# A fused encoder layer: the first scores, masks and copies of its short batch issued in another order

## The chip, the cores and the metric

The kernel runs on one core of a Trainium2 chip. The metric is the time of one execution in microseconds (us) on the device. Three executions of the kernel before took 2205.14, 2201.33 and 2206.42 us; the median is 2205.14. The profile was taken in another execution, of 2202.51 us; its span, from the first to the last instruction of the program, is 2200.7 us.

Five engines appear in the profile. PE multiplies matrices (PEld is its loading of weights, which runs beside it). DVE, ACT and POOL work on tiles element by element. SP issues DMAs, and POOL issues some of them too. The order of the instructions of an engine is fixed when the program is built.

## The reference, cut to what matters

One encoder layer runs on two batches with the same weights: 1024 tokens (called A below) and 512 tokens (called B). Per batch:

```
h = rms_norm(x, pre_w);  cols = h @ w_in            # 12304 columns
y_m = o * headnorm(mlstm_fwd + mlstm_bwd) * silu(z)   # 4 heads x 256
y_a = mix of 3 dilated window attentions * silu(z)    # 3 groups x 8 heads x 64
merged = sig(g_A) * (y_m @ w_pm) + sig(g_B) * (y_a @ w_pa)
y = x + rms_norm(merged @ w_out, post_w)
```

The mLSTM is linear attention with gates, here cut into chunks of 128 tokens. For a chunk the reference forms the scores `q k^T`, multiplies them by `exp` of a log weight under a triangular mask, multiplies by `v`, and divides by a row sum. It does so forwards and backwards for each head.

## The kernel before

All data are float32. A product is made of three matmuls (`mm3`, L212 to L214) on operands of the type float32r: each operand x is stored as a high part `hi`, a rounded copy made by ACT, and a low part `lo = x - hi`, made by DVE or POOL. The product is hi\*hi + hi\*lo + lo\*hi. Wherever a matmul needs a new operand, two instructions on two other engines come ahead of it, one after the other.

**Stages.** The program goes through the projections of A (to about 960 us in the trace), then through five stages, each of which has its own small matmuls and a stream of big ones beside it. The stages are the mLSTM of A (`mlstm`), the attention of A (`attend`), the mLSTM of B (`quad`, from about 1587 to 1775 us), the attention of B, and the end. The big matmuls (tile `dense`) belong to projections of B and to the output products of A and B. They are handed out by `Fill`: `fill(share)` issues so many steps, and a step is one `mm3` over 512 columns. `fill.stage(steps, shares)` sets the rate at the start of a stage as steps divided by shares. For `quad` there are 192 steps (`STEPS[2]`). Eight steps use one weight tile, which was split into `wh` (ACT, L275) and `wl` (DVE, L281) two units ahead, in `split_w`. `self.held` is a list of instructions behind which these splits are queued.

**Who sets the order.** PE's order is written out by hand in all of the program, SP's in the five later stages. ACT, DVE and POOL get theirs from a scheduler that simulates the program when it is built, and takes instructions by its own times and by program order. `tc.issue_after(x)` queues the block's instructions of x's engine behind x on that engine; it is no wait between engines.

**The first projection** (`value_group` with g = 0, and `combos`). A matrix product of halves is arranged in seven products (Strassen's way). The first, `m1`, has four PSUM banks; `put(B21, k)` makes the operand of the second for k = 0 to 3: transposes on PE (L423), a high copy on ACT (L430), and a `rest()` that lets PE subtract the high part in PSUM (L436) and ACT copy what remains (L437). When `m1` is done, ACT copies its four banks to `u2[t]` (L588), and the second product is added onto the same banks.

**The mLSTM of B** (`quad`). B has four chunks per head. There are 32 rounds (h, i, d): four heads, four positions, two directions. All scores between chunks of a head are kept in `st`: `prepare(h)` first copies q into `qs` as high and low part (L1321, L1322), splits the keys of chunk 0 into `kh` (ACT, L1314) and `kl` (DVE, L1315), and then, for each chunk c, multiplies (`sc`, six matmuls), splits the next chunk's keys and copies the scores to `st` (L1330). The tiles `kh` and `kl` have one buffer each.

`front(k)` makes the operand of round k: POOL masks a row of logs (L1351, `affine_select`), ACT takes `exp` (L1353), DVE multiplies by scores (L1358, L1359), ACT makes the high part `sch` (L1366) and POOL the low part `scl` (L1367). In between, POOL carries forward the products of the column factors, `cols` (L1364), which read the same row tile `rw`, loaded by a DMA that POOL issues (L253). `core(k)` multiplies with v (`num`, L1380 the high part, L1383 the low one) and normalises. Backwards rounds (d = 1) start with the last chunk, so round 1 of a head needs the scores of chunk 3.

The opening of `quad` is, in program order: `fill(2)`; `prepare(0)` from end to end with `fill(1/5)` after each of its five parts; `front(0)`; then the rounds. Round k calls, in this order, the next part of `prepare` of the next head if one is under way, the row loads, `front(k+1)`, a share of fill, and `core(k)`, which holds two more shares. Preparing the next head begins in the fourth round of a head, so its four score products stand in the fifth to the eighth round.

**The attention of A** (`attend`) has 12 units of 8 rounds. The loads of the next unit are put in a list at the second round of a unit; `spread(n)` sets how many of them each round's `tick` issues on SP, so that the list is empty after n rounds; n is 7.

Of the kernel before, what the change touches and what calls it, by code (L numbers as in the profile page):

```python
# [22 lines left out]
F32 = mybir.dt.float32  # L23
# [160 lines left out]
class Net:  # L184
# [182 lines left out]
    def combos(self, ps, H, xt, r, junk, pw, plus, minus, again, diag):  # L367
# [47 lines left out]
        def put(m, k):  # L415

            if m == T4 and k == 0:
                again()
            p = banks.pop((B21, k)) if m == B22 else ps.tile([P, BLK], F32, name="d")
            banks[m, k] = p  # L420
            begun = m in turned
            for t in range(4) if begun else ():
                nc.tensor.matmul(p[:, t * P:(t + 1) * P], turned[m][t][:, k * P:(k + 1) * P], self.ident, is_transpose=True,  # L423
                                 start=t == 0, stop=True, skip_group_check=True)
            for of, one in others.get(m, ()):
                for x in range(2):
                    nc.tensor.matmul(p, one, H[x][of][:, k], start=not begun, stop=True, skip_group_check=True)
                    begun = True
            hi, lo = H[0][m][:, k], H[1][m][:, k]
            nc.scalar.activation(hi, p, AF.Copy)  # L430
            if m not in (B21, B22):
                self.low = nc.vector.tensor_sub(lo, p, hi.bitcast(F32))  # L432
                return None

            def rest():
                nc.tensor.matmul(p, minus, hi, start=False, stop=True, skip_group_check=True)  # L436
                nc.scalar.activation(lo, p, AF.Copy)  # L437
            return rest

        return lead, norm, sub, put  # L440
# [11 lines left out]
    def value_group(self, g, T, H, sb, us, co, ps, late=None, begin=None, u3=None, more=None, turn=None):  # L452
# [70 lines left out]
        if g == 0:  # L523
# [61 lines left out]

            m1 = product(B11, w11, with_m1(), True)
            for t in range(4):
                nc.scalar.activation(u2[t], m1[t][:, :VW], AF.Copy)  # L588
            w12 = low.pop(0)
            with self.tc.issue_after(low[0]):  # L590
                last = self.sums(wa, wb, s)
# [684 lines left out]
    def quad(self, T, fill, steps, first, after, beside):  # L1276
# [10 lines left out]
        with ExitStack() as stack:  # L1287
# [15 lines left out]
            hacc = x0[:, :n * 256].rearrange("p (n c) -> p n c", c=256)  # L1303
            G = x0[:, 2 * S:4 * S].rearrange("p (c s) -> p c s", c=2)
            qs = [z.rearrange("p (c s) -> p c s", c=2) for x in [self.take("X1")] for z in (x[:, :2 * S], x[:, 2 * S:4 * S])]
            fill.stage(steps, lead + len(rounds) + n // 4 + late + 3)

            def prepare(h):
                self.need(("qk", h))
                x = head[h]  # L1310
                def keys(c):
                    k = x["k"][:, :, c * P:(c + 1) * P]
                    kk = [sb.tile([P, 2, P], F32R, name=z, bufs=1) for z in ("kh", "kl")]
                    nc.scalar.activation(kk[0], k, AF.Copy)  # L1314
                    nc.vector.tensor_sub(kk[1], k, kk[0].bitcast(F32))  # L1315
                    return kk

                with ExitStack() as st_:
                    for z in self.behind if h == 0 else self.acc[:1]:
                        st_.enter_context(self.tc.issue_after(z.ins))  # L1320
                    nc.scalar.activation(qs[0], x["q"], AF.Copy)  # L1321
                    nc.vector.tensor_sub(qs[1], x["q"], qs[0].bitcast(F32))  # L1322
                    kk = keys(0)
                yield
                for c in range(n):
                    p = psum("sc")
                    for ct in range(2):
                        self.mm3(p, [z[:, ct] for z in kk], [z[:, ct] for z in qs], ct == 0, ct == 1)
                    kk = keys(c + 1) if c < n - 1 else None
                    self.turned = nc.scalar.activation(st[h % 2][:, c], p, AF.Copy)  # L1330
                    yield

# [9 lines left out]
            def front(k):  # L1342
# [5 lines left out]
                scores = lambda c1: st[h % 2][:, c1, c * P:(c + 1) * P]  # L1348
                rm = sb.tile([P, n, P], F32, name="rm", bufs=1)[:, :i + 1]
                sg = 1 if d == 0 else -1  # L1350
                nc.gpsimd.affine_select(out=rm[:, i], in_=rw[:, 0], pattern=[[sg, P]], compare_op=OP.is_ge, fill=-NEG, base=0,  # L1351
                                        channel_multiplier=-sg)
                nc.scalar.activation(rm[:, i], rm[:, i], AF.Exp, scale=-1.0, bias=of(0, c))  # L1353
                if i == 0:
                    col[d] = sb.tile([P, 4], F32, name=f"cols{d}")
                for j in range(i):
# [3 lines left out]
                if 0 < i < n - 1:  # L1360
                    e = P - 1 if d == 0 else 0
                    for j in range(i):
                        w = of(1, chunk(j)) if j == i - 1 else col[d][:, j:j + 1]
                        nc.gpsimd.tensor_tensor(col[d][:, j:j + 1], w, rw[:, 1, e:e + 1], op=OP.mult)  # L1364
                hi, lo = (sb.tile([P, n, P], F32R, name=x)[:, :i + 1] for x in ("sch", "scl"))
                nc.scalar.activation(hi, rm, AF.Copy)  # L1366
                nc.gpsimd.tensor_sub(lo, rm, hi.bitcast(F32))  # L1367
                made[k] = hi, lo, of(2, c), [chunk(j) for j in range(i + 1)]

# [52 lines left out]
                rows(0, d)  # L1422
            self.need(("v", 0))
            load_G(0)
            fill(lead)
            for _ in prepare(0):
                fill(1 / 5)
            front(0)
            hold, coming = self.turned, None
            for k, (h, i, d) in enumerate(rounds):  # L1430
                self.tick()
# [19 lines left out]
                    load_G(h)  # L1451
                fill(1 / 3)
                core(k)
                self.sum = self.acc[1]
                next(beside, None)
            self.scans = []
# [327 lines left out]
    def attend(self, T, fill, steps, first, banks, outs, after=None, beside=None, at=()):  # L1784
# [5 lines left out]
        with ExitStack() as st:  # L1790
# [55 lines left out]
            for i in range(12):  # L1846
                now = coming
                for j, t in enumerate(now):
                    if j == 1:
                        if i < 11:  # L1850
                            coming = ready(i + 1)
                            self.spread(T.n - 1 if i or T.n > 4 else 1)
                        elif after:
                            after()
                            self.spread(T.n + 1)
# [629 lines left out]
```

## Time and profile before

| | |
|---|---|
| median of three executions | 2205.14 us (2201.33 to 2206.42) |
| the profiled execution | 2202.51 us |
| its span | 2200.7 us |
| mean granted clock of TensorE | 0.998 |
| DVE, ACT, POOL busy | 66%, 49%, 32% of the span |
| matmuls | 11962 |
| HBM read, written | 274.70 MB, 113.44 MB |

The profile's times are counted from the start of the span. In a timeline a row gives the start, the duration, the engine, the line of the kernel, the operation, the tiles (written <- read), partitions by elements with types, how many instructions were merged, and in brackets how long the engine had been idle before and what ended that. Matmuls overlap: the duration of one (0.39 us at 512 columns) is longer than the distance from its start to the start of the next (0.23 us), so the distance between starts is what a matmul costs. A stretch of several matmuls is thus read by its starts.

### The profile page before, as it was taken

The numbers are of one execution on the slowest core, as the hardware profiler recorded it, in microseconds if no ns is written. First come the engines' busy times: TensorE is split into PE (matmuls) and PEld (weight loads), VectorE is DVE, ScalarE is ACT, GpSimd is POOL, SyncE is SP. The second block draws the span as 40 slices with busy tenths as digits, with TensorE's granted clock in tenths as the row PEclk, the third lists the DMA queues.
The fourth block names the chain that finished last, engine by engine and source line by source line (L and its number), as shares of the span: only waits on it lengthen the run. The fifth ranks groups of instructions, "written<-read, shape, count | busy, mean of one in ns | idle before, by whom it ended". The sixth has DMA issues, their size and how long they took to land.

```text
span 2200.7 us, 34421 instructions
## 1 busy us (share of the span) xinstructions
PE 2181.6 (99%) x11962; PEld 1885.7 (86%) x11962; DVE 1463.0 (66%) x2970; ACT 1087.8 (49%) x2246; POOL 700.6 (32%) x994
## 2 busy tenths in 40 slices
PE   9999999999999999999999999999999999999998
PEld 8999888888888888888888889998778888888887
DVE  7765565657787555547888765564667845666673
ACT  7322243344444343446777666666755544554332
POOL 1000432333333222326677640011044422232331
PEclk9999999999999999999999999999999999999999
DMA  3742443423333222366746569996778786776773
GB/s 126 195 115 78 154 166 134 172 105 115 106 115 113 76 79 96 134 237 218 224 154 215 150 196 251 250 240 192 213 225 274 242 268 209 230 254 189 236 240 106
DMA packets 207641, 390.43 MB, mean 177 GB/s; under 512 B 37513, under 2 KB 121161, under 8 KB 207466
## 3 DMA queue, kind: packets, MB, share of 16 engines
q1 hardware_dynamic: 176584, 276.15, 39.9%
q0 software_dynamic: 27280, 99.48, 14.3%
q10 hardware_dynamic: 3602, 12.59, 1.4%
q8 instruction: 95, 1.56, 0.3%
q14 instruction: 80, 0.66, 0.1%
HBM read 274.70 MB, written 113.44 MB: 176 GB/s over the span
## 4 chain that ended last, share of the span: by engine, by line
PE 92%; DMA 3%; DVE 2%; issue 1%; ACT 1%; SPq 0%; POOL 0%; DVEq 0%; POOLq 0%; ACTq 0%
PE d L214 14%; PE d L212 14%; PE d L213 14%; PE dense L212 12%; PE dense L214 11%; PE dense L213 11%; PE lg L1678 2%; PE pt L1708 1%; PE o L1751 1%; PE num L212 1%; PE num L214 1%; PE num L213 1%; PE num L1380 1%; PE a L1096 1%; PE kv L212 1%
## 5 line engine op out<-in xcount | busy, mean ns | idle before, releaser
L212 PE MATMUL dense<-H,wh 128*128 128x512 f32 x664 | 269.9, 407 | 0.0
L214 PE MATMUL dense<-H,wl 128*128 128x512 f32 x664 | 261.2, 393 | 0.0
L213 PE MATMUL dense<-H,wh 128*128 128x512 f32 x664 | 261.1, 393 | 0.0
L214 PE MATMUL d<-Hh,phla 128*128 128x512 f32 x608 | 236.7, 389 | 0.0
L212 PE MATMUL d<-Hh,phla 128*128 128x512 f32 x608 | 236.7, 389 | 0.0
L213 PE MATMUL d<-Hl,phla 128*128 128x512 f32 x608 | 236.7, 389 | 0.0
L281 DVE TENSOR_TENSOR wl<-wraw,wh 128x1024 fp32r<-128x1024 f32 (+1 forms) x121 | 149.8, 1240 | 58.4 <-ACT wh L275 58.3
L214 PE MATMUL d<-Hh,phlb 128*128 128x512 f32 x456 | 177.5, 389 | 0.0
L212 PE MATMUL d<-Hh,phlb 128*128 128x512 f32 x456 | 177.5, 389 | 0.0
L213 PE MATMUL d<-Hl,phlb 128*128 128x512 f32 x456 | 177.5, 389 | 0.0
L275 ACT ACTIVATE wh<-wraw 128x1024 fp32r<-128x1024 f32 (+1 forms) x124 | 128.3, 1036 | 68.3 <-PE dense L213 25.1
L214 PEld LDWEIGHTS dense<-H,wl 128*128 128x128 f32 x664 | 125.1, 188 | 28.1
L696 POOL TENSOR_TENSOR psum_w<-pw_raw 128x512 f32<-128x512 f32 x38 | 57.3, 1508 | 277.5 <-DMA pw_raw<-w_in 254.2
L214 PE MATMUL d<-vhi,Hl 128*128 128x322 f32 x448 | 140.6, 314 | 0.5 <-DVE Hl L432 0.3
L212 PE MATMUL d<-vhi,Hh 128*128 128x322 f32 x448 | 140.4, 313 | 0.1
L212 PEld LDWEIGHTS dense<-H,wh 128*128 128x128 f32 x664 | 125.6, 189 | 16.7 <-issue 1.2
L213 PE MATMUL d<-vlo,Hh 128*128 128x322 f32 x448 | 139.7, 312 | 0.0
L213 PEld LDWEIGHTS dense<-H,wh 128*128 128x128 f32 x664 | 125.8, 189 | 14.9
L214 PEld LDWEIGHTS d<-Hh,phla 128*128 128x128 f32 x608 | 114.2, 188 | 23.7
L213 PEld LDWEIGHTS d<-Hl,phla 128*128 128x128 f32 x608 | 114.2, 188 | 23.6
L212 PEld LDWEIGHTS d<-Hh,phla 128*128 128x128 f32 x608 | 114.2, 188 | 23.6
L1697 DVE CUSTOM_DVE_ANT_0 ls<-lg,bias 128x256 f32<-128x256 f32 (+2 forms) x240 | 78.7, 350 | 79.1 <-PE lg L1678 52.8
(635 smaller groups left out, 5807.5 us busy)
## 6 DMA issues: line engine op xcount, KB each, us to landing
pw_raw<-w_in SPq DMA_DIRECT2D x76, 512.0 KB, 4.1
wraw<-w_in SPq DMA_DIRECT2D x63, 512.0 KB, 4.6
aqk_a<-pwk SPq DMA_DIRECT2D x40, 512.0 KB, 3.3
wraw<-w_pm POOLq DMA_DIRECT2D x24, 512.0 KB, 5.7
wraw<-w_out POOLq DMA_DIRECT2D x24, 512.0 KB, 3.9
aqk_b<-sw SPq DMA_DIRECT2D x40, 256.0 KB, 5.2
wraw<-w_v POOLq DMA_DIRECT2D x22, 430.0 KB, 6.6
qk_a<-pwk SPq DMA_DIRECT2D x16, 512.0 KB, 2.6
```

The source lines that it names most:

```text
L212: nc.tensor.matmul(out, lh, rh, start=start, stop=False, **kw)
L213: nc.tensor.matmul(out, lh, rl, start=False, stop=False, **kw)
L214: nc.tensor.matmul(out, ll, rh, start=False, stop=stop, **kw)
L275: high = nc.scalar.activation(hi[:, :n], raw[:, :n], AF.Copy)
L281: low = (self.lows or nc.vector).tensor_sub(lo[:, :n], raw[:, :n], hi[:, :n].bitcast(F32))
L696: self.nc.gpsimd.tensor_add(s[:, 0], ws[1][:, 0], ws[1][:, 1])
L1096: nc.tensor.matmul(p[:, c - c0], kT[:, ct, c * P:(c + 1) * P], qT[:, ct, c * P:(c + 1) * P], start=ct == 0, stop=ct == 1)
L1380: nc.tensor.matmul(pn, hi[:, j], z[:, c1], start=j == 0 and z is v[0], stop=False)
L1678: nc.tensor.matmul(lg[:, hh], q[hh][:, qs], z.rearrange("p (n j) -> p n j", j=P)[:, pair], start=z is k[hh], stop=z is not k[hh])
L1697: nc.vector.tensor_tensor_reduce(out=ls[rows, hh], in0=ts["lg"][hh][rows, of], in1=bt[rows, hh, by], scale=1.0, scalar=NEG, op0=OP.add, op ...
L1708: nc.tensor.transpose(pp[:, hh * nk + x], ts["ls"][:, hh, x * P:(x + 1) * P], self.ident)
L1751: nc.tensor.matmul(of(hh, 0, P), vh(kt[x], hh), pt[:, hh * len(kt) + x], start=x == 0, stop=x == len(kt) - 1)
```

## The change

- In `combos` and `value_group`: the copies of banks 1 to 3 of `m1` are queued on ACT behind the last low copy of B21; that of bank 0 is left free.
- In `quad`, `prepare` is taken apart. `kh` has two buffers (the pool's own number), `kl` keeps one, and the high part of the next keys is queued ahead of a chunk's matmuls instead of behind them. For heads 1 to 3 an empty round is put in, so that the four score products stand in rounds 6, 7 and 8 of a head and in round 1 of the next.
- For head 0 the opening is now: first part of `prepare`; `fill(2 + 3/5)`; scores of chunk 0; `fill(1/5)`; `front(0)`; the three other chunks with `fill(1/5)` after each; `fill(1)`; then the rounds. From `front(0)` to the end of the first `core`, the weight splits are queued behind the `exp`, the product and the high part of `front(0)` (`self.held`). The stage's shares are 42 instead of 41.
- In `front`, the column products (L1364) are queued on POOL behind the mask (L1351) of the same front.
- In `attend` for A, the loads of the next unit are spread over 6 rounds instead of 7 (for B, as before).

```diff
-                nc.scalar.activation(lo, p, AF.Copy)
+                self.copied = nc.scalar.activation(lo, p, AF.Copy)
...
             for t in range(4):
-                nc.scalar.activation(u2[t], m1[t][:, :VW], AF.Copy)
+                with self.tc.issue_after(self.copied.ins) if t else ExitStack():
+                    nc.scalar.activation(u2[t], m1[t][:, :VW], AF.Copy)
...
-            fill.stage(steps, lead + len(rounds) + n // 4 + late + 3)
+            fill.stage(steps, lead + len(rounds) + n // 4 + late + 4)
...
-                def keys(c):
-                    k = x["k"][:, :, c * P:(c + 1) * P]
-                    kk = [sb.tile([P, 2, P], F32R, name=z, bufs=1) for z in ("kh", "kl")]
-                    nc.scalar.activation(kk[0], k, AF.Copy)
-                    nc.vector.tensor_sub(kk[1], k, kk[0].bitcast(F32))
-                    return kk
+                of = lambda c: x["k"][:, :, c * P:(c + 1) * P]
+                def high(c):
+                    k = sb.tile([P, 2, P], F32R, name="kh")
+                    nc.scalar.activation(k, of(c), AF.Copy)
+                    return k
+                def low(c, hi):
+                    k = sb.tile([P, 2, P], F32R, name="kl", bufs=1)
+                    nc.vector.tensor_sub(k, of(c), hi.bitcast(F32))
+                    return hi, k
...
-                    kk = keys(0)
+                    kk = low(0, high(0))
                 yield
+                if h:
+                    yield
                 for c in range(n):
+                    coming = high(c + 1) if c < n - 1 else None
                     p = psum("sc")
                     for ct in range(2):
                         self.mm3(p, [z[:, ct] for z in kk], [z[:, ct] for z in qs], ct == 0, ct == 1)
-                    kk = keys(c + 1) if c < n - 1 else None
+                    kk = coming is not None and low(c + 1, coming)
                     self.turned = nc.scalar.activation(st[h % 2][:, c], p, AF.Copy)
                     yield
...
-                nc.gpsimd.affine_select(...)
-                nc.scalar.activation(rm[:, i], rm[:, i], AF.Exp, scale=-1.0, bias=of(0, c))
+                select = nc.gpsimd.affine_select(...)
+                self.fronts = [nc.scalar.activation(rm[:, i], rm[:, i], AF.Exp, scale=-1.0, bias=of(0, c))]
...
-                        nc.gpsimd.tensor_tensor(col[d][:, j:j + 1], w, rw[:, 1, e:e + 1], op=OP.mult)
+                        with self.tc.issue_after(select.ins):
+                            nc.gpsimd.tensor_tensor(col[d][:, j:j + 1], w, rw[:, 1, e:e + 1], op=OP.mult)
...
-                nc.scalar.activation(hi, rm, AF.Copy)
+                self.fronts += [*self.state, nc.scalar.activation(hi, rm, AF.Copy)]
...
-            fill(lead)
-            for _ in prepare(0):
+            scores = prepare(0)
+            next(scores)
+            fill(lead + 3 / 5)
+            next(scores)
+            fill(1 / 5)
+            front(0)
+            self.held = self.fronts
+            for _ in scores:
                 fill(1 / 5)
-            front(0)
+            fill(1)
...
                 core(k)
+                self.held = []
...
-                            self.spread(T.n - 1 if i or T.n > 4 else 1)
+                            self.spread(T.n - (2 if T.n > 4 else 1) if i or T.n > 4 else 1)
```

More of the change, by code (lines that the diff above doesn't have):

```diff
@@ L1350, in front @@
                 sg = 1 if d == 0 else -1
-                nc.gpsimd.affine_select(out=rm[:, i], in_=rw[:, 0], pattern=[[sg, P]], compare_op=OP.is_ge, fill=-NEG, base=0,
-                                        channel_multiplier=-sg)
-                nc.scalar.activation(rm[:, i], rm[:, i], AF.Exp, scale=-1.0, bias=of(0, c))
+                select = nc.gpsimd.affine_select(out=rm[:, i], in_=rw[:, 0], pattern=[[sg, P]], compare_op=OP.is_ge, fill=-NEG, base=0,
+                                                 channel_multiplier=-sg)
+                self.fronts = [nc.scalar.activation(rm[:, i], rm[:, i], AF.Exp, scale=-1.0, bias=of(0, c))]
                 if i == 0:
```

## The prediction

> **What bounds the kernel now.** I read the page first, then the list of who PE waited for, then PE's timeline where these waits lie, then the other engines there.
>
> ```profile
> PE 2181.6 (99%) x11962; PEld 1885.7 (86%) x11962; DVE 1463.0 (66%) x2970; ACT 1087.8 (49%) x2246; POOL 700.6 (32%) x994
> ```
>
> PE is busy in 2181.6 of 2200.7 us, and the change neither adds nor removes a matmul. So it can only save time in which PE stands still or runs slowly, and can only lose time by making PE stand still. PE's longest waits are these (in all, times, longest):
>
> ```profile
> PE num L1380 <- issue: 3.8, 1, 3.8
> PE d L436 <- ACT Hh L430: 0.8, 2, 0.5
> PE sc L214 <- DVE kl L1315: 0.7, 1, 0.7
> PE sc L212 <- ACT kh L1314: 0.4, 1, 0.4
> ```
>
> Three of the four lie in the opening of `quad`, the fourth in the first projection. The timeline of PE shows where:
>
> ```profile
> 1593.60 0.39 PE L214 MATMUL dense<-H,wl 128*128 128x512 f32 x1
> 1594.34 0.50 PE L212 MATMUL sc<-X,kh 128*128 128x512 f32 x1 [0.35 <-ACT kh L1314]
> 1594.68 0.39 PE L213 MATMUL sc<-X,kh 128*128 128x512 f32 x1
> 1595.75 0.50 PE L214 MATMUL sc<-X,kl 128*128 128x512 f32 x1 [0.67 <-DVE kl L1315]
> ...
> 1604.74 0.39 PE L214 MATMUL dense<-H,wl 128*128 128x512 f32 x1
> 1608.91 0.48 PE L1380 MATMUL num<-V0a,sch 128*128 128x258 f32 x2 [3.78 <-issue]
> ...
> 1610.76 0.63 PE L213 MATMUL dense<-H,wh 128*128 128x512 f32 x1
> 1611.18 0.63 PE L214 MATMUL dense<-H,wl 128*128 128x512 f32 x1
> ```
>
> Distances between starts are what counts. Undisturbed it is 0.23 us (0.227 over many). Before the first `sc` it is 0.74, before the first use of `kl` 1.07, and before the first `num` 4.17: excesses of 0.51, 0.84 and 3.94 us. After the hole two neighbours are 0.42 us apart, so PE then runs at half speed. The windows (length, then busy time by engine, then PEclk, the granted clock) show for how long:
>
> ```profile
> 1609.40:1613.00 3.60, 3.60 (x11) 2.83 (x11) 1.96 (x13) 1.60 (x5) 1.40 (x7) 0.54 1.04 390
> 1613.00:1775.00 162.00, 162.00 (x852) 137.80 (x851) 124.32 (x312) 87.91 (x196) 76.11 (x136) 1.00 0.73 231
> ```
>
> A clock of 0.54 over 3.60 us loses 1.66 us that the list of waits doesn't name. From 1613 to the end of the stage PE is busy all of the 162 us at full clock. The opening of `quad` thus holds 0.51 + 0.84 + 3.94 + 1.66 = **6.95 us**, and the rest of that stage nothing.
>
> **Why the hole is there.** The first `num` waits for a chain over three engines:
>
> ```profile
> 1603.13 0.60 ACT L1330 ACTIVATE st<-sc 128x512 f32<-128x512 f32 x1 [1.37 <-PE sc L214]
> 1604.94 1.06 ACT L275 ACTIVATE wh<-wraw 128x1024 fp32r<-128x1024 f32 x1 [1.21 <-PE dense L213]
> 1606.38 0.39 ACT L1353 ACTIVATE rm<-rm,col 128x128 f32<-128x128 f32 x1
> 1607.77 0.29 DVE L1359 TENSOR_TENSOR rm<-rm,st 128x128 f32<-128x128 f32 x1
> 1608.52 0.29 ACT L1366 ACTIVATE sch<-rm 128x128 fp32r<-128x128 f32 x1
> 1608.89 0.46 POOL L1367 TENSOR_TENSOR scl<-rm,sch 128x128 fp32r<-128x128 f32 x1 [11.74 <-ACT sch L1366]
> ```
>
> The work of the chain itself is 0.39 + 0.29 + 0.29 + 0.46 us. But `front(0)` stands behind the last score copy, and a weight split and other work of the dense stream come between its links. It needs only the scores of chunk 0, which were copied 6 us earlier.
>
> **The change, part by part.**
>
> *Opening of `quad`.* The rate falls from 192/41 = 4.68 to 192/42 = 4.57 steps per share; a step is three matmuls, 0.68 us. Ahead of the scores of chunk 0, 2.2 shares made 10 steps; now 2.6 shares make 12. PE comes there 1.36 us later, at 1595.2 instead of 1593.8, and to its third matmul, the first with `kl`, at 1595.6.
>
> ```profile
> 1593.88 0.41 ACT L1314 ACTIVATE kh<-Q 128x256 fp32r<-128x256 f32 x1
> 1595.28 0.42 DVE L1315 TENSOR_TENSOR kl<-Q,kh 128x256 fp32r<-128x256 f32 x1
> 1595.06 1.62 POOL L253 DMA_DIRECT2D rw<-rw_b  x3 [18.19 <-DVE wl L281]
> 1596.68 0.30 POOL L1351 TENSOR_SCALAR_AFFINE_SELECT rm<-rw 128x128 f32<-128x128 f32 x1
> ```
>
> At unchanged times `kh` is there at 1594.29 and `kl` at 1595.70, so 0.1 us would be left of the 1.35; and since both now come ahead of the dense stream's instructions in program order, I count it as nothing: **-1.35**. From the end of chunk 0's scores (about 1596.6) to the first `num`, PE has 10 steps (one after each chunk, four for `fill(1)`, two for the round's third) and 18 score matmuls: 6.8 + 4.1 = 10.9 us. The mask stands at 1596.68 behind row loads that waited for a weight split; even so the rest of the chain took 6.2 us in all its queueing before (1603.13 to 1609.35), and from 1596.98 would end at 1603.2, 4 us early. So the hole goes, **-3.94**, and with it the slow clock, **-1.66**. What is late next is round 1, which needs chunk 3: its scores end near 1603, its `num` comes 10 steps and some small matmuls later, about 7.5 us, again more than 6.2. Queueing the splits behind `front(0)` delays one, at step 16, which is used 16 steps (11 us) after; and the front is done long before. Nothing.
>
> The Trainium skill, page "TensorE: Matmul & The Clock Gate", part 1 on the HAM clock gate, says that the array falls to half clock after an idle window of about 3.4 us, and that the windows run freely. Its length and the half rate agree with the rows above. As the idle time was 3.78 us, a whole window fits in it only at some phases, so executions could differ, and by that page the 1.66 us would be missing in most: an estimate of -5.6 in place of -7.25.
>
> *A second `kh`, `kh` ahead of the matmuls, an empty round.* In heads 1 to 3 the old single `kh` cost PE nothing (162 of 162 us busy). The late point is the backward round 0 of the next head, which needs chunk 3. So it ran before, for head 1:
>
> ```profile
> 1642.97 0.39 PE L214 MATMUL sc<-X,kl 128*128 128x512 f32 x1
> 1645.05 0.51 ACT L1403 ACTIVATE hn<-X,r 128x256 f32<-128x256 f32 x1 [0.94 <-POOL r L1402]
> 1645.46 0.58 ACT L1330 ACTIVATE st<-sc 128x512 f32<-128x512 f32 x1
> 1646.15 0.29 DVE L1359 TENSOR_TENSOR rm<-rm,st 128x128 f32<-128x128 f32 x1 [1.97 <-ACT st L1330]
> 1647.37 0.31 ACT L1366 ACTIVATE sch<-rm 128x128 fp32r<-128x128 f32 x1
> 1653.77 0.40 PE L1380 MATMUL num<-V1a,sch 128*128 128x258 f32 x2
> ```
>
> The scores ended at 1643.36, `sch` at 1647.68, 4.3 us later, and `num` needed it at 1653.77, so 6.1 us were spare. A round later, the six score matmuls stand at 1647.4 to 1649.2, and 4.6 us remain: 0.3 more than the chain took. Between 0 (the chain runs as it did) and about 2.1 us a head (another split of 1.06 us on ACT and one that long on DVE come between); I take 0, the nearest row.
>
> *Column products behind the mask.* They are on POOL and 0.2 us each; PE waited for no POOL result in this stage after the hole. Nothing either way, as long as `scl` isn't held.
>
> *Copies of `u2`.*
>
> ```profile
> 21.27 1.41 ACT L588 ACTIVATE u<-d 128x322 f32<-128x322 f32 x4
> 22.54 0.63 ACT L430 ACTIVATE Hh<-d 128x512 fp32r<-128x512 f32 x1
> 25.16 0.51 PE L436 MATMUL d<-Hh,Hl 128*128 128x512 f32 x1 [0.47 <-ACT Hh L430]
> 27.52 0.44 ACT L599 ACTIVATE u2b<-d 128x322 f32<-128x322 f32 x1 [1.22 <-PE d L214]
> ```
>
> Four copies in a row hold up the second `Hh`; its transposes end at 22.2. With one copy ahead of it, it starts near 22.25 instead of 22.54: **-0.3**. The other three (1.05 us) fit in ACT's idle 1.22 us before 27.52, and bank 1 is wanted only 12 matmuls into the second product. Bounds: 0, if DVE, not PE, sets the pace there, to the 0.8 us in the list.
>
> *Loads of `attend`.*
>
> ```profile
> 1300.00:1587.00 287.00, 287.00 (x2190) 259.25 (x2189) 171.14 (x720) 188.69 (x571) 30.18 (x57) 1.00 0.85 229
> SPq L253 <- PE o L1609: 6.4, 2, 4.7
> ```
>
> PE is never idle there, though a load made SP wait 4.7 us. Nothing.
>
> **Sum**: -1.35 - 3.94 - 1.66 - 0.3 = -7.25 us against 2202.51 us of the profiled execution, so 2195.3. The median of the three runs is 2.6 us above that execution; the forecast for the median is **2198 us**.
>
> **Rivals.**
>
> 1. *The hole stays*, because `front(0)` is queued late or its mask waits for the rows: then only 0.3 to 1.7 us are gone, 2203.5 to 2205. For it: POOL's order is the scheduler's, and it waited 18 us in front of the row loads. Against: 4 us of spare time. Chance 0.13.
> 2. *The hole shrinks* to 2 or 3 us, perhaps without the slow clock: about 2201. Chance 0.1.
> 3. *The slow clock was this one execution's*: most runs had none to lose, and the gain is 7.25 - 1.66 = 5.6 us, so 2205.1 - 5.6 = 2199.5. For it: only one execution is profiled. Against: in that one the clock fell. Chance 0.05. The rule of the page named above makes this the usual case.
> 4. *Slower*: the scores of chunk 3 come too late in heads 1 to 3. The place is the backward round 0 of each head, the price what the chain takes over 4.6 us, three times. It decides from 7.25 / 3 = 2.4 us a head, a chain of 7.0 us instead of 4.3. If it makes holes like the one removed, 3.94 + 1.66 each, it costs 16.8 us: 2198 + 16.8 = 2215. Against: DVE is busy 124 of 162 us there, ACT 88. Chance 0.12.
>
> **Chances.** The forecast has 0.6, with a range of its own from 2194 to 2201 (the scatter of the runs is 5 us). The range reaches up to the first rival: 2194 to 2206; beyond lie rival 4 and the forecast's lower edge. About 0.2% (4.4 us) is what a measurement of this kernel can tell from no change. Faster by over that, under 2200.7: 0.63, from the forecast but for its upper edge and rivals 2 and 3 in part. Within: 0.25, from rivals 1 and 2 and the edges. Slower: 0.12, rival 4.
>
> **What would show it.** Right: `num` at L1380 leaves the list of waits, the granted clock stays at 1.00 through the opening of `quad`, `sc` no longer waits for `kh` or `kl`, and the stage is 7 us shorter. Wrong: a wait of `num` or `scl` in the second round of a head, a lower clock there, or new waits of PE for DMAs in the attention of A.

## The result, and the profile after

| | before | after |
|---|---|---|
| median (10 runs each) | 2207.77 us (2201.33 to 2211.85) | 2200.6 us (2196.68 to 2202.71) |
| ratio of the runs | | 0.9969, 95% interval 0.9959 to 0.9979 |
| profiled execution | 2202.51 us | 2196.68 us |
| its span | 2200.7 us | 2194.8 us |

The change makes the kernel faster by 0.31%, 4.6 to 9.1 us at 95%. The longer series of before has a higher median than the three runs that the prediction started from. So the level came out 2.6 us above the 2198 forecast, while the step was the one forecast: 7.25 us worked out, 7.2 us between the medians. With an interval from 4.6 to 9.1 us, agreement as close as that is partly luck.

The list of who PE waited for, in the profile after (in all, times, longest), now holds of the four rows shown before only two, both shorter (its first row, a wait for a load at the start of the program, stood in before with 3.1 us):

```profile
PE d L2254 <- DMA Hh<-prew: 3.3, 1, 3.3
PE dense L214 <- DVE H L2114: 0.6, 1, 0.6
PE d L436 <- ACT Hh L430: 0.5, 1, 0.5
PE lg L1695 <- DMA V0b<-aqk_a: 0.4, 1, 0.4
PE sc L214 <- DVE kl L1321: 0.3, 1, 0.3
...
PE num L1390 <- ACT sch L1376: 0.2, 1, 0.2
```

`num <- issue` and `sc <- kh` are gone, and the wait for `kl` that is left isn't in the opening but at 1638.70. (Lines have moved: `num` is L1390 and L1393, `front` L1360 to L1377, `kh` L1316, `kl` L1321.) PE's timeline of the opening of `quad`:

```profile
1596.07 0.39 PE L212 MATMUL sc<-X,kh 128*128 128x512 f32 x1
1596.29 0.39 PE L213 MATMUL sc<-X,kh 128*128 128x512 f32 x1
1596.63 0.50 PE L214 MATMUL sc<-X,kl 128*128 128x512 f32 x1
...
1603.56 0.39 PE L214 MATMUL sc<-X,kl 128*128 128x512 f32 x1
...
1608.55 0.40 PE L1390 MATMUL num<-V0a,sch 128*128 128x258 f32 x2
...
1611.66 0.40 PE L1390 MATMUL num<-V0a,sch 128*128 128x258 f32 x2
```

The first `sc` starts without a bracket, so without a wait. Before the first use of `kl` the distance is 0.34 us instead of 1.07; the 0.11 us above the usual 0.23 are what the prediction left over there. The chain of `front(0)`, in the timelines of POOL, ACT and DVE:

```profile
1597.57 0.30 POOL L1360 TENSOR_SCALAR_AFFINE_SELECT rm<-rw 128x128 f32<-128x128 f32 x1
1601.62 0.46 POOL L1377 TENSOR_TENSOR scl<-rm,sch 128x128 fp32r<-128x128 f32 x1 [3.75 <-ACT sch L1376]
```

```profile
1600.00 0.58 ACT L1339 ACTIVATE st<-sc 128x512 f32<-128x512 f32 x1
1600.48 0.39 ACT L1362 ACTIVATE rm<-rm,col 128x128 f32<-128x128 f32 x1
1601.23 0.31 ACT L1376 ACTIVATE sch<-rm 128x128 fp32r<-128x128 f32 x1 [0.36 <-DVE rm L1368]
...
1604.77 1.05 ACT L275 ACTIVATE wh<-wraw 128x1024 fp32r<-128x1024 f32 x1
```

The `exp` stands behind the score copy of chunk 1, not behind that of chunk 3, and the weight split `wh` comes after `sch`. The operand is complete at 1602.08 and needed at 1608.55: 6.5 us to spare, where the prediction had 4. The windows (length, busy time by engine, granted clock) show the place where PE before stood for 3.78 us and then ran at 0.54:

```profile
1604.00:1609.00 5.00, 5.00 (x24) 4.18 (x23) 3.19 (x8) 3.29 (x7) 1.85 (x4) 1.00 0.17 48
1609.00:1613.00 4.00, 4.00 (x20) 3.35 (x19) 1.93 (x9) 2.84 (x7) 2.21 (x5) 1.00 1.01 304
```

PE is busy all the time at a clock of 1.00. In the first projection, one copy to `u2` now stands ahead of the second `Hh`, the other three behind the last `Hl` (ACT's timeline, L589):

```profile
20.56 0.43 ACT L589 ACTIVATE u<-d 128x322 f32<-128x322 f32 x1
21.51 0.60 ACT L430 ACTIVATE Hh<-d 128x512 fp32r<-128x512 f32 x1 [0.52 <-PE d L423]
...
25.15 1.10 ACT L589 ACTIVATE u<-d 128x322 f32<-128x322 f32 x3
```

**Where the time went.** Both kernels have the same 11962 matmuls, so the traces can be laid side by side: the start of the matmul of the same number from the start, at places where the order of both agrees. These are the differences after minus before, by stretch, worked out from PE's timelines:

| stretch | us |
|---|---|
| first 12 us | -0.71 |
| 12 to 24 us (copies of `u2`) | -0.35 |
| attention of A | +1.92 |
| opening of `quad` (to about 1623 in before) | -6.36 |
| the rest of heads 0 to 3 (called heads 1 to 3 below) | +0.55 |
| end of `quad`, start of the attention of B | +0.16 |
| attention of B and the end | -1.21 |
| sum, with +0.02 between the projections | -5.98 |

Two things help to read it. The rows for the attention of A and for the end, and the first 12 us, are stages whose time differs between executions of the same code, as the experiments show. And the border between the opening and the rest of the heads cuts the two kernels at the same number of matmuls, but not at the same matmuls: up to there the changed kernel has done six `dense` more (0.23 us each) and six `num` fewer (0.115 us each), which is 0.67 us of work and no standing time. Without it the opening is 7.0 us shorter, and the rest of the heads 1.2 us longer.

### The profile page after: what moved, and what is told of

It reads as the page before. It is cut to its first block, busy times and chain, and to the rows that moved or that the text cites. A ratio compares the mean times of both kernels' runs of the same rounds, so it can differ in the third digit from the quotient of the medians.

```text
span 2194.8 us, 34409 instructions
## 1 busy us (share of the span) xinstructions
PE 2180.1 (99%) x11962; PEld 1883.1 (86%) x11962; DVE 1460.9 (67%) x2970; ACT 1088.8 (50%) x2246; POOL 706.5 (32%) x994
## 4 chain that ended last, share of the span: by engine, by line
PE 90%; DMA 4%; DVE 2%; issue 1%; ACT 1%; POOL 1%; SPq 0%; DVEq 0%; POOLq 0%; ACTq 0%
PE d L214 14%; PE d L212 14%; PE d L213 14%; PE dense L212 11%; PE dense L214 11%; PE dense L213 11%; PE lg L1695 1%; PE pt L1725 1%; PE num L212 1%; PE num L214 1%; PE num L213 1%; PE o L1768 1%; PE num L1390 1%; PE a L1097 1%; PE kv L212 1%
## 5 line engine op out<-in xcount | busy, mean ns | idle before, releaser
L281 DVE TENSOR_TENSOR wl<-wraw,wh 128x1024 fp32r<-128x1024 f32 (+1 forms) x121 | 150.1, 1241 | 49.3 <-ACT wh L275 49.0
```

What stands on the lines that cost most here:

```text
L281: low = (self.lows or nc.vector).tensor_sub(lo[:, :n], raw[:, :n], hi[:, :n].bitcast(F32))
```

## The experiments

Each kernel is named with the parts that it has. "Ratio" is to the kernel before, run on the same chip. Below, the table of all kernels by the same stretches, from one profile each. In all kernels with the new opening the column of the opening holds the same 0.67 us of work, so -6.24 to -6.36 there means some 7.0 us of standing time, and heads 1 to 3 cost 0.67 us more than is printed:

| kernel | copies | attention of A | opening | heads 1 to 3 | ratio (95%) |
|---|---|---|---|---|---|
| changed kernel | -0.35 | +1.9 | -6.36 | +0.6 | 0.9969 (0.9959 to 0.9979) |
| e1_opening | 0.0 | +2.9 | -6.24 | +3.1 | 0.9987 (0.9977 to 0.9997) |
| e2_rest | -0.38 | +3.8 | -0.21 | +3.1 | 1.0008 (0.9997 to 1.0018) |
| e3_spread7 | -0.37 | +3.5 | -6.35 | +0.1 | 0.9975 (0.9965 to 0.9986) |
| e4_noround | -0.32 | +1.6 | -6.36 | +3.8 | 0.9985 (0.9975 to 0.9995) |
| e5_held | 0.0 | +7.5 | -0.47 | +0.9 | 0.9999 (0.999 to 1.0008) |
| e6_noheld | -0.32 | +2.2 | -6.36 | +0.7 | 0.9972 (0.9962 to 0.9982) |
| e7_notie | -0.36 | +4.7 | -6.36 | +0.9 | 0.9969 (0.9958 to 0.9979) |
| e8_u2 | -0.38 | +2.1 | +0.97 | 0.0 | 0.9996 (0.9987 to 1.0004) |
| e9_early | -0.33 | +3.1 | -6.36 | +3.0 | 0.9991 (0.9981 to 1.0001) |
| e10_after_early | -0.38 | +7.4 | -6.36 | +0.3 | 0.9975 (0.9965 to 0.9985) |
| e11_allearly | -0.36 | +7.5 | -6.36 | +1.7 | 0.9978 (0.9969 to 0.9987) |
| e12_allearly_round | -0.31 | +2.6 | -6.32 | +1.1 | 0.9969 (0.9957 to 0.9981) |

### The new opening alone, and everything but it

e1_opening is before with the new order of the opening and the held splits, nothing else:

```diff
...
-            fill(lead)
-            for _ in prepare(0):
-                fill(1 / 5)
-            front(0)
+            scores = prepare(0)
+            next(scores)
+            fill(lead + 3 / 5)
+            next(scores)
+            fill(1 / 5)
+            front(0)
+            self.held = self.fronts
+            for _ in scores:
+                fill(1 / 5)
+            fill(1)
...
```

> The kernel before with the new opening of quad alone (order of prepare, fill and front for head 0, splits queued behind front(0), 42 shares); one kh, no empty round, no tie, old copies, old spread. If the gain is the hole and the slow clock of the opening: 6.0 to 7.0 us faster than before, granted clock 1.00 through the opening, no wait at the first num. If the second kh is needed for it: waits of sc for kh of 0.3 us or more after each chunk, and less than 5 us of gain. If the gain comes from the other parts: under 2 us.

e2_rest is the changed kernel with the old opening, 41 shares and no held splits:

> The changed kernel with the old opening of quad; all else as changed. If the gain is the opening's: the hole of some 3.9 us before the first num and a clock near 0.5 behind it are back, and the time is that of the kernel before less 0.3 us for the copies, within 1.5 us. If the other parts carry it: 3 us faster or more.

Measured: with the new opening alone the stretch is 6.24 us shorter; with everything else it is 0.21 us shorter and the hole stands as before, in e2_rest's list of waits:

```profile
PE num L1390 <- issue: 3.8, 1, 3.8
PE num L1390 <- ACT X L1400: 1.7, 2, 1.5
PE sc L214 <- DVE kl L1321: 0.7, 1, 0.7
```

So the hole, the waits for `kh` and `kl` and the slow clock belong to the order of the opening; in e1_opening, with one `kh`, the new order shows no wait for it. But e1_opening as a whole gains only 0.13%, less than half of the changed kernel: it loses 3.1 us again in heads 1 to 3, by the same count. There PE waits for `kl` three times (list of waits of e1_opening):

```profile
PE sc L214 <- DVE kl L1315: 1.6, 3, 0.9
PE num L1380 <- ACT X L1390: 0.3, 1, 0.3
```

This the prediction had not seen coming. e2_rest loses 3.1 us there too, half of it at one `num` that waits 1.5 us for ACT (second row). Just before it ACT had stood for 3.26 us, until 1705.87, for the loads of head 3, and what was queued behind the copy of q came late. In this profile, then, the rest of the change costs time under the old opening; the ratio of e2_rest, 1.0008, can't be told from 1.

### The loads of head 1 behind a moved weight load

The timelines of SP's queue, of before and then of the changed kernel, show what lies behind it:

```profile
1595.68 3.76 SPq L253 DMA_DIRECT2D Q<-qk_b  x4
1599.89 1.77 SPq L253 DMA_DIRECT2D V1a<-vs_b  x2
1605.13 1.27 SPq L228 DMA_DIRECT2D qk_b<-sw  x1
1607.28 0.34 SPq L264 DMA_DIRECT2D wraw<-w_in  x1
```

```profile
1594.75 0.37 SPq L228 DMA_DIRECT2D qk_b<-sw  x1
1607.11 0.33 SPq L264 DMA_DIRECT2D wraw<-w_in  x1
...
1609.29 2.52 SPq L253 DMA_DIRECT2D Q<-qk_b  x4
```

In before the loads of q and k for head 1 (`Q`) are issued ahead of the weight load `wraw`. The new opening calls `fill(1)` ahead of the rounds, and the steps that it issues carry a weight load with them, which now stands ahead of the head's loads. It can only be issued when DVE has split the weight that lies in the buffer (the changed kernel's timeline of DVE):

```profile
1605.85 1.23 DVE L281 TENSOR_TENSOR wl<-wraw,wh 128x1024 fp32r<-128x1024 f32 x1 [0.66 <-ACT wh L275]
```

The split ends at 1607.08 and the load follows at 1607.11; SP issues nothing from 1595.1 on, and the loads of head 1 come 13.6 us later than in before. The copy of q (ACT), which in before waits for nothing, then waits for them (in this order: before, the changed kernel, e1_opening):

```profile
1617.34 1.05 ACT L1321 ACTIVATE X<-Q 128x1024 fp32r<-128x1024 f32 x1
```

```profile
1618.95 1.06 ACT L1327 ACTIVATE X<-Q 128x1024 fp32r<-128x1024 f32 x1 [2.66 <-DMA Q<-qk_b]
```

```profile
1620.13 1.06 ACT L1321 ACTIVATE X<-Q 128x1024 fp32r<-128x1024 f32 x1 [1.14 <-DMA Q<-qk_b]
```

The changed kernel could bear it because its first scores come one empty round later. e4_noround is the changed kernel without that round:

```diff
-                if h:
-                    yield
```

> The changed kernel without the empty round in prepare, so that heads 1 to 3 get their scores one round earlier, as before. PE lost 1.2 us from the second head on in the changed kernel. If the later scores cause that (rival 4 in small): these waits (0.5 us at sc for kl, 0.3 us at num for sch) go, and it is 0.5 to 1.2 us faster than the changed kernel. If the empty round is needed for something else in the change: new waits in rounds 4 to 8 of a head.

Measured: opening unchanged, heads 1 to 3 +3.8 us instead of +0.6, and four waits for `kl`:

```profile
PE sc L214 <- DVE kl L1321: 2.0, 4, 0.9
```

The empty round, counted at nothing in the prediction, is thus worth about 3 us under the new opening. The timed runs agree in sum: the six kernels that have the new opening and the round come to ratios from 0.9969 to 0.9975, the four without the round to 0.9978 to 0.9991, though the intervals of single kernels overlap. No run takes out the second `kh` alone. e9_early keeps the round out and issues the loads of head 1 behind `front(0)`, ahead of the moved fill:

```diff
             self.held = self.fronts
+            head[1] = self.ml_load(T, 1)
+            self.need(("qk", 1))
             for _ in scores:
...
                     if h < 3:
-                        head[h + 1] = self.ml_load(T, h + 1)
+                        if h:
+                            head[h + 1] = self.ml_load(T, h + 1)
...
```

> The changed kernel without the empty round, with the loads of head 1 issued right behind front(0) of head 0, ahead of the weight load on SP. Without the empty round, PE lost 0.56 us at the first scores of head 1, and 3.8 us in heads 1 to 3. In all kernels with the new opening SP stood 12 us at a weight load that now comes ahead of head 1's loads, which were issued 13 us later than before. If that is the cause: head 1's loads are issued before 1600 us, its q copy doesn't wait for a DMA, and the wait for kl at its first scores goes; heads 2 and 3, whose loads stand as before, keep their waits. If it is the pace of the other engines: the wait for kl at head 1 stays.

Measured: the loads are issued at 1595.97 again, and at head 1 `sc` no longer waits for `kl`. But heads 2 and 3 keep their waits, and the sum is still +3.0 us, so the loads behind the weight load account for no more than 0.8 of the 3.8 (e9_early's timeline of PE, at head 2):

```profile
1665.73 0.50 PE L214 MATMUL sc<-X,kl 128*128 128x512 f32 x1 [0.80 <-DVE kl L1321]
...
1667.89 0.99 PE L1388 MATMUL num<-V1a,sch 128*128 128x258 f32 x6 [0.28 <-ACT X L1398]
...
1672.83 0.50 PE L214 MATMUL sc<-X,kl 128*128 128x512 f32 x1 [0.36 <-DVE kl L1321]
```

Its loads for head 2 also stand directly behind a weight load, at 1653.85 (1652.62 in before), though PE is 3.3 us earlier there in these profiles, and about 6 us earlier counted from the start of `quad`; the copy of q ends a wait of 4.56 us for them at 1661.65 (2.36 us, at 1659.26, in before). e11_allearly therefore issues those of heads 2 and 3 a round earlier as well:

```diff
...
+                if h in (1, 2) and i == d == 0:
+                    head[h + 1] = self.ml_load(T, h + 1)
+                    self.need(("qk", h + 1))
                 if i == 0 and d == 1:
                     if h < 3:
-                        if h:
-                            head[h + 1] = self.ml_load(T, h + 1)
                         self.spread(1)
...
```

> This is the changed kernel without the empty round, with the loads of q and k for head 1 issued behind front(0) and those for heads 2 and 3 issued one round earlier than in before. Theory (heads 1 to 3 lose 3 us without the empty round because q and k arrive too late for a PE that is 6 us earlier): the loads of heads 2 and 3 are issued some 5 us earlier, the copies of q no longer wait for a DMA just ahead of the scores, and heads 1 to 3 cost between 0 and +1 us against before instead of +3.0 to +3.8; the ratio to before is about 0.997, as for the changed kernel. Rival (the loss is in the chain over ACT and DVE behind the loads, with one buffer of kl): the loads land earlier, but sc goes on waiting for kl and heads 1 to 3 still cost 2 us or more; ratio about 0.9985.

Measured: it falls between the two. No copy of q waits for a DMA any more, and heads 1 to 3 cost +1.7 us, a little over half of what they cost in e9_early; the ratio, 0.9978, also lies between those of e4_noround and the changed kernel, within the intervals of both. `sc` goes on waiting for `kl`:

```profile
1675.89 0.50 PE L214 MATMUL sc<-X,kl 128*128 128x512 f32 x1 [0.49 <-DVE kl L1321]
...
1687.97 0.50 PE L214 MATMUL sc<-X,kl 128*128 128x512 f32 x1 [0.30 <-DVE kl L1321]
```

So late loads explain about 2.1 of the 3.8 us of e4_noround (0.8 at head 1, 1.3 at heads 2 and 3), as far as single profiles tell. Of what is left, waits for `kl` are 0.8 us; in e12_allearly_round, with the empty round, one of 0.3 us remains. The trace shows what holds up `kl` in e11_allearly: at both places `kh` was ready in time (at 1673.93 and 1680.72), but DVE, without a pause, first did other work that its order puts ahead. Before 1687.51, when it began with `kl`, that was a weight split of 2.05 us (L281, from 1684.24) and two instructions on `K` (L1946, 1.38 us).

e10_after_early and e12_allearly_round ask whether the changed kernel, which has the empty round, still pays for its late loads. Both have the spread of 7; e10_after_early has the early loads of head 1, e12_allearly_round those of all heads.

> This is the changed kernel with two edits: the loads of attend spread over 7 rounds as before, and the loads of head 1 issued right behind front(0), ahead of fill(1). Theory (the moved fill(1) puts a weight load ahead of head 1's loads on SP, and the empty round covers that delay): the loads of head 1 are issued some 12 us earlier than in the changed kernel (about 1597 instead of 1609), but since the empty round covered the delay already, PE gains at most the 0.5 us that heads 1 to 3 still cost there; opening -6.3 us against before, heads 1 to 3 between 0 and +0.6, time within 2 us of the changed kernel. Rival (the delay costs more than the empty round hides): heads 1 to 3 become 1 us or more shorter than in before, and the time is 2 us or more under the changed kernel.

> This is the changed kernel with the empty round kept, the loads of attend spread over 7 rounds as in before, and the loads of q and k issued early for all heads (head 1 behind front(0), heads 2 and 3 one round earlier). Theory (the empty round already covers what late loads cost, so that earlier loads have nothing left to save): opening -6.3 us, heads 1 to 3 between 0 and +0.6, time within 2 us of the changed kernel. Rival (late loads still cost something in the changed kernel): heads 1 to 3 become shorter than in before by 0.5 us or more.

Measured: 2201.39 and 2200.17 us, heads 1 to 3 at +0.3 and +1.1. Earlier loads save nothing that can be told where the empty round is in. Neither beats the changed kernel (2200.6, and by its ratio 0.9969) beyond the scatter; none of these versions does.

### The held splits

e5_held is before with `self.held` set between `front(0)` and the end of the first `core`, in the old order; e6_noheld is the changed kernel without it:

```diff
-            self.held = self.fronts
```

> The kernel before with one thing of the opening: from front(0) to the end of the first core the weight splits are queued behind front(0)'s exp, product and high part. The order of prepare, fill and front is the old one. If the hole is made by the splits that come between the links of the chain: it shrinks from 3.9 us to under 1 us, the clock stays at 1.00 behind it, and the opening is 4 to 5 us shorter. If it is the place of front(0) behind all the scores: the hole stays above 2.5 us.

> The changed kernel without the queueing of splits behind front(0). From the end of chunk 0's scores to the first num there were 11.1 us in the changed kernel, and the high and low part were ready 6.5 us ahead of it. If that is cover enough: the opening is as in the changed kernel within 0.3 us. If not: a wait at the first num again.

Measured in e5_held: with no split between its links the chain is shorter, but the hole only shrinks, and the clock falls all the same (a row of its list of waits, then its windows):

```profile
PE num L1380 <- issue: 2.4, 1, 2.4
```

```profile
1613.00:1615.20 2.20, 0.72 (x4) 0.71 (x5) 0.62 (x2) 1.75 (x3) 0.67 (x2) 1.00 1.07 384
1615.20:1618.60 3.40, 3.40 (x11) 2.64 (x10) 2.85 (x9) 1.36 (x5) 2.20 (x6) 0.50 0.80 230
```

The wait of 2.41 us lies between the two outcomes stated ahead (under 1 us, over 2.5 us), nearer to the second: the splits were the smaller part of the hole, some 1.4 us; the place of `front(0)` behind all scores was the larger. The stretch as a whole came out only 0.47 us shorter.

In e6_noheld the opening is as short as in the changed kernel, and its ratio is the same within the intervals. The traces show why: in both kernels every engine does the same instructions in the same order, so in the new opening the queueing of the splits moves nothing. e6_noheld is thus a second profile of the changed kernel, and says how far two profiles of one program differ: 0.2 us in heads 1 to 3, 0.3 us in the attention of A, and some 3 us from there to the end, 1.7 of which are half clock (last section).

### Copies, column products and loads

A tie is an `issue_after`. e8_u2 is before with the tie of the copies alone, e7_notie the changed kernel without the tie of the column products, e3_spread7 the changed kernel with `self.spread(T.n - 1 ...)` in `attend`, as before:

> The kernel before with the copies of banks 1 to 3 queued behind the last low copy, and nothing else. Expected: 0.35 us between the start and the second product, no other difference that the time can show; the opening of quad with its hole as before. It is also a second look at the attention of A, whose code is that of the kernel before: all five profiles since show PE 1.6 to 3.8 us later there than the first profile did. If that is scatter of DMA landings, it is 1 to 4 us later here too; if it came from the changes of each of those kernels, it is within 0.5 us of the first profile.

> This is the changed kernel without the tie of the column products behind the mask on POOL. Theory (the tie is worth nothing either way, for PE waits for nothing of POOL in this stage): opening -6.3 us against before, heads 1 to 3 between 0 and +0.8, time within 2 us of the changed kernel. Rival (the tie is what lets the masks come early): the mask of round 0, or masks of later rounds, come later behind column products, num or scl appear in PE's list of waits, and the opening or heads 1 to 3 lose 1 us or more.

> The changed kernel with the loads of the attention of A spread over 7 rounds as before. PE lost 1.9 us in that stage of the changed kernel, at three waits for loads. If the spread is the cause: these waits are back at the size of the kernel before (0.2 us each), and the kernel is 1.5 to 2 us faster than the changed one, 8.5 to 9 us faster than before. If it is the scatter of DMAs from execution to execution: waits of 0.2 to 0.7 us at the same or other loads, and no difference in time that can be told.

Measured, e8_u2: -0.38 us at its place, and -0.31 to -0.38 in every kernel with the tie of the copies, 0.0 in the two without; too little for a timed ratio to show.

e7_notie: the ratio is that of the changed kernel. The tie does do what it says. Without it column products come ahead of `scl` on POOL and wait for their rows:

```profile
1601.19 0.31 POOL L1360 TENSOR_SCALAR_AFFINE_SELECT rm<-rw 128x128 f32<-128x128 f32 x1
1601.46 0.19 POOL L1373 TENSOR_TENSOR cols<-col,rw 128x1 f32<-128x1 f32 x1
1605.44 0.19 POOL L1373 TENSOR_TENSOR cols<-col,rw 128x1 f32<-128x1 f32 x1 [3.79 <-DMA rw<-rw_b]
1606.27 0.19 POOL L1373 TENSOR_TENSOR cols<-col,rw 128x1 f32<-128x1 f32 x1 [0.64 <-DMA rw<-rw_b]
1606.41 0.46 POOL L1376 TENSOR_TENSOR scl<-rm,sch 128x128 fp32r<-128x128 f32 x1
```

From the mask to the start of `scl` it is 5.2 us here and 4.05 us in the changed kernel. That 1.2 us lies inside the 6.5 us to spare, so PE doesn't see it.

e3_spread7: the attention of A costs +3.5 us with the old spread and +1.9 with the new, and the ratios overlap. The other rows of the table show that this is scatter: e1_opening, e5_held and e8_u2 have before's code in that stage and came to +2.9, +7.5 and +2.1. There PE waits for loads in some executions and not in others; in e10_after_early, with before's spread too:

```profile
1456.07 0.38 PE L1698 MATMUL lg<-V0a,Q 128*128 128x256 f32 x1 [2.52 <-DMA V0a<-aqk_a]
1457.20 0.39 PE L1698 MATMUL lg<-V0b,Q 128*128 128x256 f32 x1 [0.75 <-DMA V0b<-aqk_a]
```

Where such waits bring the clock down (last section), that adds to it: in e5_held and e11_allearly 6.83 us at half clock follow them. The profiled execution of before had no such wait in this stage, which may be part of why its time lay below the later median.

## Why the prediction was right

*Opening: 6.95 predicted, 7.0 measured (6.36 by the table, and 0.67 us of work that stands on its wrong side).* Right in all steps: the hole, both waits and the slow clock are gone together, and only in kernels with the new order. The 0.1 us left before `kl` was counted at nothing; the excesses over the usual distance between starts add up to 7.2 us in before's opening, a little more than the 6.95 read off, and 0.2 us in the changed kernel's.

*The chain of `front(0)`.* Predicted done 4 us ahead of its `num`, in fact 6.5; rival 1 (the hole stays) and rival 2 (it shrinks) are out. Round 1, named as the next to be late, had its scores at 1603.95 and its `num` at 1611.66: 7.7 us, where 7.5 were worked out.

*The slow clock (rival 3).* Not this execution's alone: e2_rest and e8_u2 have the same 3.78 us of waiting for `num`, and each was followed by a low clock (0.50 from 1610.92 to 1614.33 in e2_rest, and from 1609.13 to 1615.95 in e8_u2). The Trainium skill, page "TensorE: Matmul & The Clock Gate", part 1 on the HAM clock gate, read as the prediction read it, would have let most such executions escape, since a whole free-running window of about 3.4 us would have to be idle. Here the measurement decides against that: e5_held shows the half clock even after 2.41 us, and the last section shows what was enough.

*Copies of `u2`: 0.3 predicted, about 0.35 measured.* Right.

*Column products, held splits, loads of `attend`: nothing.* Right as to time. For the held splits the reason was another than the one given: the prediction took them to delay one split, and they move none. In the attention of A the new waits for DMAs that the prediction named as a sign of being wrong did appear (0.4 and 0.2 us), but kernels with before's code there have them too.

*The empty round and the second `kh`: nothing, or up to 2.1 us a head lost (rival 4).* Here the step failed, though the sum didn't show it. The prediction weighed the empty round as a delay of chunk 3's scores against the 6.1 us to spare. It didn't ask what a PE that comes 7 us earlier finds in heads 1 to 3: loads of q and k that are not earlier (and at head 1 come 13.6 us later, behind the weight load that `fill(1)` put into SP's queue), and a DVE that is still busy when `kl` is wanted. Without the empty round, 2.3 to 4.5 us of the 7.0 are given back there (+1.7 to +3.8 in the table's count, four kernels); with it 0.7 to 1.7 us (+0.1 to +1.1, six kernels). So rival 4's place, heads 1 to 3, was right; its cause was the wrong one (late loads and `kl`, not a late chain behind chunk 3), and the part of the change that it blamed is the one that holds the loss down. The loss that stays is in no term of the sum: the stage came out 5.8 us shorter, where the prediction's sign of being right was 7. That the total agreed all the same is in part luck: the interval from 4.6 to 9.1 us holds the 6.2 us that the stage and the copies make together just as well. What part the second `kh` has in this stays open.

*The list of waits.* The rows called PE's longest left out the second and third of before's list: 3.1 us at the start of the program, before PE's first matmul, and 0.9 us at 2101.57, in the last stage. The change touches neither, so the sum is as it was; but the second is 0.2 us in the profile after, which is part of the -1.21 in the table, and it is back in e11_allearly (1.1) and e12_allearly_round (0.9).

*The level.* The median of three runs was taken as the base; ten runs gave 2.6 us more. That moved the forecast's level, not the step.

## What to carry to other kernels

When a share of background work is moved to an earlier place, look through every queue that it feeds: here the matmuls were harmless, but the weight load that came with them was put ahead of other loads on SP, waited there for a split on another engine, and held them for 13.6 us. What that cost was small here, at most 0.8 us by single profiles. Time saved at the start of a stage can be given back later in it, where loads keep their old times while PE comes earlier; some slack in the order, such as a round between loading and use, is what keeps the gain. A part that seems to do nothing by the profile of before should be judged together with the part whose side effect it may cover. And where two kernels are compared by the numbers of their matmuls, check that the same matmuls lie on both sides of a border.

## What the runs showed of the hardware that was not expected

The granted clock fell to half after less idle time than before's profile suggested, and for longer at times. In e5_held above, one wait of 2.41 us was followed by 3.40 us at 0.50. In e10_after_early the two waits for loads shown above, 2.52 and 0.75 us, lie on both sides of 1455.02 (windows: length, busy time by engine with PE first, granted clock):

```profile
1451.61:1455.02 3.41, 1.94 (x11) 1.68 (x9) 2.23 (x11) 1.87 (x6) 0.00 (x0) 1.00 1.04 214
1455.02:1458.43 3.41, 1.61 (x9) 1.40 (x10) 0.71 (x5) 0.00 (x0) 0.00 (x0) 1.00 0.95 308
1458.43:1461.84 3.41, 3.41 (x14) 3.23 (x13) 0.77 (x5) 1.09 (x4) 0.00 (x0) 0.50 0.89 170
```

These windows are cut where the clock can change. In all 14 traces the granted clock changes only at ticks 3.41 us apart; in before, 468 such steps lie between the first rise and the fall. Twelve times it fell while the program ran. The step that ended with the fall always held 1.52 to 3.40 us in which PE stood (in the second window 3.41 - 1.61 = 1.80 us). Steps at full clock in which it stood for up to 1.47 us (the first window) were not followed by a fall. Idle time adds up within a step, so in e6_noheld two waits of 0.97 and 0.82 us, at 1816.84 and 1818.16, were enough. Where the ticks lie differs between executions, so a tick may split a short hole over two steps, and it escapes. By this reading the hole of 3.78 us can't, since at least 1.89 us of it fall into one step.

The half clock lasted one step, or two where PE stood for 0.8 to 1.6 us in the first of them (elsewhere 0.4 us at most). That is what happened in e8_u2 behind the unchanged hole, and why its opening came out 0.97 us longer:

```profile
1609.13:1615.95 6.82, 5.62 (x15) 4.61 (x16) 3.78 (x16) 2.92 (x8) 3.41 (x10) 0.50 0.90 325
```

So a hole on PE costs its own length and, if it fills enough of a step, 1.7 us more for each step of half clock that PE works through. The border between 1.47 and 1.52 us is read off these traces, in which the ends of matmuls are modelled; no run was made to test it.
